# Hyena's convolution chain: the elementwise work on one engine, two butterfly levels summed in PSUM, and the channels in halves

## The chip, the cores and the metric

The kernel runs on one core of a Trainium2 chip. The metric is the device time of one execution in microseconds. Three runs of the kernel before gave 2783.18, 2772.97 and 2788.09 us, so its median is 2783.18 us. One more execution was taken with the hardware profiler, and all rows below come from it.

TensorE multiplies matrices into PSUM banks. VectorE (DVE in the rows), GpSimd (POOL) and ScalarE (ACT) do the elementwise work, and SyncE (SP) issues most loads. A tile of 128 partitions by 1024 fp32 numbers is the usual unit.

## What is computed

The reference is a trunk of two layers over 1024 tokens with 1024 channels. Layer 0 adds two mixers, a Hyena long convolution and a differential attention with rotary positions; layer 1 is a gated position mixer; each layer ends with a feed-forward part with a short convolution. The change concerns the Hyena part and, in one table, the rotary products:

```python
def hyena_mix(proj, ...):                       # proj: 1024 x 1536
    v, x1, x2 = jnp.split(dwconv3(proj, conv_w, conv_b), 3, axis=-1)
    filt = hyena_filters(L, w1, b1, freq, w2, b2, w3)   # 2 orders, 2L taps, 512 channels
    z = v
    for o, gate in enumerate((x1, x2)):
        z = gate * fftconv_bidir(z, filt[:, o], d_skip[o])
    return z
# fftconv_bidir: y = irfft(rfft(u, 2L) * rfft(h, 2L))[:L]
```

So two convolutions stand in a row for each channel, and the second needs the gated result of the first.

## The kernel before, in words

The function `layer0_front` holds all of it, from the start to the first scores of the attention at about 675 us. Its TensorE work is of two kinds: projections (`conv_mtile` for Hyena's three inputs, `proj_v`, `proj_kc`, `proj_qk`), which take each fp32 operand as a high and a low part (tiles `hh`, `hl`, `whi`, `wlo`, results in `pj`), and Fourier matmuls in plain fp32 (tables `tbf` forward, `tbi` inverse, results in `pf`). A plain fp32 matmul shows as two records in the trace.

A transform over 2048 points is split in two: an 8-point butterfly over tile rows `r`, and 128-point matmuls. `dft` does the forward one: 16 matmuls, a level of sums and differences out of PSUM (one ScalarE copy, then an addition and a subtraction on VectorE for each of the real and imaginary part `c`), and two further levels on SBUF tiles `f`. `spectrum` multiplies by the filter's spectrum, loaded from DRAM. `idft` does three levels of sums and differences and returns two tiles `q0`, `q1`; `conv_chain` then runs the inverse matmuls on them and multiplies by the gate. `conv_chain(half)` does this for order 0 and order 1, for 256 channels at a time, so that there are four such steps, called chain steps here. `filters` makes the eight filter parts (order x half of the channels x direction) with `dft_part` and stores their spectra.

Strings such as `F_DFT`, `F_INV`, `F_PART`, `F_SP` and `F_ROPE` give the engine of each elementwise operation in turn, V for VectorE and G for GpSimd. `F_W` does so for the low parts of the weights (`wlo`). The helpers `add`, `sub` and `mul` show as line 132 in the profile, `stt` (a scaled addition) as 128, `mm` as 154.

`eager(main(), side())` fixes the order in which the work is written down: `side` (all filters, then the chain of both halves) goes on until it lacks an input, then `main` (the projections: v, context keys, Hyena's, queries and keys) goes on by one unit. A scheduler then orders each engine's instructions by readiness, and what stands under `first()` goes ahead. The tiles come from pools: seven buffers of the 2048-column tiles `f`, two of the PSUM tiles `pj` and two of `pf`.

Of the kernel before, what the change touches and what calls it, by code (L numbers as in the profile page):

```python
# [20 lines left out]
P = 128  # L21
# [19 lines left out]
F_DFT, F_INV = ("VGVGVVVGVVVGVGVVVG", "VGVGVVVGVVVGVGVVVG", "VGVGVVVGVVVGVGVVVG", "VGVGVVVGVVVGGGVVVG"), ("VGVVVVGGVGVVVGGGVVGVGVVGG", "VGVVVVGGVGVVVGGGVVGVGVVGG", "VGVVVVGGVGVVVGGGVVGVGVVGG", "VGVVVVGVVGVVVGGGVVGVGVVGG")  # L41
F_PART = ("VGGGVGGVVVVVG", "VGGVVGGVVVVVV", "VGGGVGGVVVVVG", "VGGVVGGVVVVVV", "VGGGVGGVVVVVG", "VGGVVGGVVVVVV", "VGGGVGGVVVVVG", "VGGVVGGVVVVVV")
F_SP = ("GGVVVV", "GGVVVV", "GGVVVV", "GGVVVV", "GGVVVV", "GGVVVV", "GGVVVV", "GGVVVV")
F_W = ("GGGGGGGGGGGG", "GGGG", "VGGG", "VGGVVGGG")
F_ROPE = ("GVVG", "GVVV", "GVVG", "VVVG", "GVVG", "GVVG", "GVVV", "GVGG")
# [47 lines left out]
def tile_kernel(ctx: ExitStack, tc: tile.TileContext, ap: dict, out: bass.AP, stop=None):  # L93
# [194 lines left out]
    def layer0_front(fp):  # L288
        with ExitStack() as es:
# [141 lines left out]
            def dft(z, n):  # L431

                e = turns(F_DFT[n])
                a, b = f8(), f8()
                for c in range(2):
                    g1 = fwd(z, c, 1)
                    A.copy(out=b[:, c], in_=g1)
                    g0 = fwd(z, c, 0)
                    add(V, a[:, c], g0, b[:, c])
                    sub(V, b[:, c], g0, b[:, c])  # L440
                    yield
# [63 lines left out]
            def filters():  # L505
                h2r = h2s.rearrange("p (s r) -> p r s", r=8)
                for o in range(2):
                    raw = f8()
                    w3, w3s = raw.rearrange("p a b n -> p a (b n)")[:64, 0], None
                    w3 = raw[:64, 0].rearrange("p (a b) n -> p a (b n)", a=2)  # L510
                    w3s = raw[:64, 1].rearrange("p (a b) n -> p a (b n)", a=2)
                    ld(w3, ap["hy_w3"][:, o])
                    add(V, w3s[:, 0], w3[:, 0], w3[:, 1])
                    sub(V, w3s[:, 1], w3[:, 0], w3[:, 1])
                    ws = f8(F32R)
                    w3h = ws[:, 0].rearrange("p (a b) n -> p a (b n)", a=2)
                    w3l = ws[:, 1].rearrange("p (a b) n -> p a (b n)", a=2)
                    A.copy(out=w3h[0:64], in_=w3s)
                    A.copy(out=w3h[64:128], in_=w3s)
                    sub(V, w3l[0:64], w3s, w3h[0:64])  # L520
                    sub(V, w3l[64:128], w3s, w3h[0:64])
                    for half in range(2):
                        win = h8(ap["window"][half], (1, 8))[:, 0]
                        cs = slice(half * CH, (half + 1) * CH)
                        dsk = tp.tile([P, CH], F32, tag="dsk", name=nm("dsk"), bufs=1)
                        ld(dsk[0:1], ap["dskip"][o : o + 1, cs])
                        for sd in range(2):
                            z = f8z()
                            for g in range(2):
                                ps = ps4()  # L530
                                for r in range(4):
                                    mm(ps[:, r], h2r[:, g * 4 + r], w3h[:, sd, cs], True, False)
                                    mm(ps[:, r], h2r[:, g * 4 + r], w3l[:, sd, cs], False, True)
                                gs = slice(g * 4, g * 4 + 4)
                                mul(V, z[:, gs], ps, win[:, gs])
                            if sd == 0:

                                p0 = ps2("pf")
                                mm(p0[:, :CH], h2r[:, 0], w3h[:, 1, cs], True, False)
                                mm(p0[:, :CH], h2r[:, 0], w3l[:, 1, cs], False, True)  # L540
                                f0 = tp.tile([P, CH], F32, tag="f0", name=nm("f0"), bufs=1)
                                mul(V, f0[0:1], p0[0:1, :CH], win[0:1, 0])
                                add(V, f0[0:1], f0[0:1], z[0:1, 0])
                                V.tensor_scalar(out=f0[0:1], in0=f0[0:1], scalar1=0.5, scalar2=None, op0=MUL)
                                stt(V, z[0:1, 0], dsk[0:1], 1.0 / S, f0[0:1], MUL, ADD)
                            yield
                            X = yield from dft_part(z, sd, 2 * o + half)
                            for par in range(2):
                                st(Hd[o, half, par][:, sd * 1024 : (sd + 1) * 1024],
                                   X[:, par].rearrange("p a b -> p (a b)"))  # L550
                            yield
# [20 lines left out]
            def idft(Y, n):  # L572

# [29 lines left out]
                q0, q1 = f8(), f8()  # L603
                add(e(), q0[:, :, 0], E[:, :, 0], O[:, :, 0])
                sub(e(), q1[:, :, 0], E[:, :, 0], O[:, :, 0])
                stt(V, q0[:, :, 1::2], O[:, :, 1::2], RT2, E[:, :, 1::2], MUL, ADD)
                stt(V, q1[:, :, 1::2], O[:, :, 1::2], -RT2, E[:, :, 1::2], MUL, ADD)
                add(e(), q0[:, 0, 2], E[:, 0, 2], O[:, 1, 2])
                sub(e(), q0[:, 1, 2], E[:, 1, 2], O[:, 0, 2])
                sub(e(), q1[:, 0, 2], E[:, 0, 2], O[:, 1, 2])  # L610
                add(e(), q1[:, 1, 2], E[:, 1, 2], O[:, 0, 2])
                return q0, q1

            def conv_chain(half):
# [3 lines left out]
                for o in range(2):  # L618
# [7 lines left out]
                    if o == 0:  # L626
                        xg = h8(x1d[half].rearrange("p a b -> p (a b)"), (1, 8))[:, 0]
                        z = f8z()
                        for g in range(2):
                            ps = ps4()  # L630
                            for r in range(4):
                                for c in range(2):
                                    mm(ps[:, r], tbi[:, c, g * 4 + r], q[g][:, c, r], c == 0, c == 1)
                            gs = slice(g * 4, g * 4 + 4)
                            mul(V, z[:, gs], ps, xg[:, gs])
                            yield
                    else:
# [83 lines left out]
            def proj_hyena():  # L721
# [23 lines left out]
                for half in range(2):  # L745
                    for kind in range(3):
                        for j in range(2):
                            a = conv_mtile(4 * kind + 2 * half + j)
                            if pend:
                                post(*pend)  # L750
                            pend = (half, kind, j, a)
                            yield
# [1121 lines left out]
```

## Time and profile before

| | before |
|---|---|
| median of three runs | 2783.18 us |
| the profiled execution | 2781.85 us, its span 2780.1 us |
| TensorE busy | 2488.7 us (90%) |
| VectorE busy | 1803.7 us (65%) |
| GpSimd busy | 1264.8 us (45%) |
| ScalarE busy | 1205.2 us (43%) |

The shares are means over the whole span. The front stage is the first quarter of it, and the slices, windows and timelines below show it apart. A row of a group gives line, engine, operation, the tile written and the tiles read, the shapes, the count, the busy time with the mean of one in ns, and the idle time just before them with what ended it. In a timeline the two numbers in front are start and length, and the brackets hold the idle time before and its releaser.

### The profile page before, as it was taken

To read this page: it belongs to the slowest core of one execution; us is meant where nothing else is said; L and a number is where in the kernel's file an instruction comes from. 1 tells how busy PE (TensorE), PEld (TensorE's weight loads), DVE (VectorE), ACT (ScalarE), POOL (GpSimd) and SP (SyncE) were. 2 spreads that over 40 slices of the span, in tenths; PEclk is the share of its full clock that TensorE was granted. 3 is DMA by queue.
4 is the path that set the end of the run, shared out by engine and by line. 5 is a ranking of instruction groups with operands and counts; after the bars stand their busy time and mean duration, and the time that the engine had idled before them with its cause. 6 is when DMAs were issued, how large, how long until landed. Compare 5 with 4: busy or idle time off the path is not lost. (4 is left out here: it accounts for less than half of the span.)

```text
span 2780.1 us, 30586 instructions
## 1 busy us (share of the span) xinstructions
PE 2488.7 (90%) x11192; PEld 1981.5 (71%) x11192; DVE 1803.7 (65%) x2021; ACT 1205.2 (43%) x1871; POOL 1264.8 (45%) x917
## 2 busy tenths in 40 slices
PE   6799667767988889999999999999999999999897
PEld 2798556655767766777777777778877777787676
DVE  4676787874998376656666876642367665566854
ACT  2322111113767255555555444512257565665342
POOL 1333654545444163332323776613343433338775
PEclk9899888888999989999999999999999999999998
DMA  7134131235761265788878833311335777779422
GB/s 279 65 111 158 38 121 39 90 128 181 227 188 50 73 204 129 206 206 216 217 205 227 294 121 110 113 38 48 142 88 125 175 181 170 173 160 319 144 80 99
DMA packets 166855, 412.76 MB, mean 148 GB/s; under 512 B 16011, under 2 KB 28815, under 8 KB 164528
## 3 DMA queue, kind: packets, MB, share of 16 engines
q1 hardware_dynamic: 86352, 248.76, 27.9%
q0 software_dynamic: 34848, 63.45, 13.4%
q10 hardware_dynamic: 45504, 98.58, 9.6%
q8 instruction: 88, 1.44, 0.2%
q14 instruction: 63, 0.52, 0.1%
HBM read 261.31 MB, written 85.98 MB: 125 GB/s over the span
## 5 line engine op out<-in xcount | busy, mean ns | idle before, releaser
L154 PE MATMUL b<-u,u 128*128 128x512 f32 (+1 forms) x5624 | 1331.1, 396 | 65.2 <-POOL u L132 23.8
L154 PEld LDWEIGHTS b<-u,u 128*128 128x128 f32 x5624 | 1063.1, 192 | 331.4 <-POOL u L132 34.1
L132 DVE TENSOR_TENSOR u<-u,u 128x512 fp32r<-128x512 f32 (+2 forms) x470 | 464.5, 1014 | 337.9 <-ACT u L1141 178.9
L132 POOL TENSOR_TENSOR u<-u,u 128x512 fp32r<-128x512 f32 (+1 forms) x338 | 504.6, 1514 | 298.5 <-ACT u L1141 183.9
L1152 POOL DMA_DIRECT2D u<-u x242 | 211.3, 920 | 491.9 <-ACT u L1151 378.7
L1141 ACT CAST u<-u 128x512 fp32r<-128x512 f32 x462 | 261.7, 616 | 238.6 <-DVE u L132 96.0
L154 PE MATMUL b<-x,u 128*128 128x512 f32 x1224 | 296.8, 397 | 0.8 <-DMA u<-u 0.8
L128 DVE SCALAR_TENSOR_TENSOR u<-u,cols,u 128x1023 f32<-128x1023 f32 x176 | 232.3, 1326 | 93.2 <-ACT u L1588 85.2
L154 PEld LDWEIGHTS b<-x,u 128*128 128x128 f32 x1224 | 229.5, 188 | 61.9 <-issue 3.4
L132 POOL TENSOR_TENSOR f<-f 128x256 f32<-128x256 f32 (+2 forms) x99 | 124.7, 1273 | 209.9 <-DVE f L132 180.7
L1150 ACT CAST u<-u 128x512 fp32r<-128x512 f32 x242 | 146.1, 614 | 117.7 <-DVE u L132 89.6
L1151 ACT ACTIVATE u<-u 128x512 fp32r<-128x512 f32 x242 | 149.3, 628 | 67.2 <-POOL u L132 60.3
L132 DVE TENSOR_TENSOR f<-f 128x256 f32<-128x256 f32 (+3 forms) x176 | 177.2, 1055 | 1.1
L132 DVE TENSOR_TENSOR u<-u,b 128x512 f32<-128x512 f32 (+1 forms) x132 | 112.2, 859 | 71.5 <-PE b L154 66.7
L154 PE MATMUL pj<-hh,whi 128*128 128x512 f32 x320 | 132.7, 415 | 24.2 <-DVE t L128 14.0
L1588 ACT ACTIVATE u<-u,cols 128x1024 f32<-128x1024 f32 x88 | 109.3, 1242 | 90.2 <-DVE u L132 89.4
L128 DVE SCALAR_TENSOR_TENSOR x<-b,mods,x 128x512 f32<-128x512 f32 (+1 forms) x104 | 88.7, 905 | 68.4 <-PE b L154 68.4
L154 PE MATMUL pj<-hh,wlo 128*128 128x512 f32 x320 | 130.2, 407 | 3.2 <-POOL wlo L132 1.6
L154 PE MATMUL pj<-hl,whi 128*128 128x512 f32 x320 | 131.3, 410 | 0.0
L132 POOL TENSOR_TENSOR p<-p,p 128x1280 f32<-128x1280 f32 x27 | 79.4, 2944 | 94.1 <-ACT p L885 75.3
L874 ACT ACTIVATE p<-s,nx 128x1280 f32<-128x1280 f32 x64 | 85.0, 1328 | 42.0 <-DVE nx L870 39.2
L147 ACT CAST whi<-wraw 128x1024 fp32r<-128x1024 f32 x28 | 29.3, 1049 | 160.5 <-PE pj L154 138.5
(229 smaller groups left out, 3218.3 us busy)
## 6 DMA issues: line engine op xcount, KB each, us to landing
u<-u POOLq DMA_DIRECT2D x242, 256.0 KB, 4.6
u<-wup SPq DMA_DIRECT2D x88, 512.0 KB, 4.9
Td<-u ACTq DMA_DIRECT2D x66, 512.0 KB, 5.5
u<-Td SPq DMA_DIRECT2D x56, 512.0 KB, 4.4
wraw<-modw SPq DMA_DIRECT2D x48, 512.0 KB, 5.5
u<-wdown SPq DMA_DIRECT2D x40, 512.0 KB, 6.1
wraw<-modw0b SPq DMA_DIRECT2D x32, 512.0 KB, 4.6
xs<-x ACTq DMA_DIRECT2D x48, 256.0 KB, 2.0
```

What stands on the lines that cost most here:

```text
L128: eng.scalar_tensor_tensor(out=o, in0=a, scalar=sc, in1=b, op0=op0, op1=op1)
L132: eng.tensor_tensor(out=o, in0=a, in1=b, op=op)
L147: A.copy(out=hi, in_=x)
L154: T.matmul(o, l, r, start=st and not onto, stop=sp, skip_group_check=onto)
L874: A.activation(q.p[m], q.s, AF.Exp, bias=q.nx, accum_out=q.l[:, m : m + 1])
L1141: A.copy(out=t[:, H0], in_=x)
L1150: A.copy(out=t[:, H0], in_=x)
L1151: A.activation(t[:, H1], t[:, H0].bitcast(F32), AF.Copy, scale=-1.0)
L1152: G.dma_start(out=t[:, H1], in_=x, accum_op=ADD)
L1588: A.activation(a, c, AF.Identity, bias=col(f"fb{l}", f), scale=col(f"fw{l}1", f))
```

## The change

Four things change in `layer0_front`.

First, the tables of the chain and of the rotary products name VectorE throughout. Those of the filter parts and of the weights' low parts stay.

Second, `dft` negates four of its eight input rows on ScalarE into a tile `zn`, and lets TensorE add up both terms of the first level in PSUM: 32 matmuls instead of 16, four ScalarE copies instead of two, and no additions out of PSUM. Third, `idft` no longer forms `q0` and `q1`. ScalarE scales the odd part and a negated copy of it, and the inverse matmuls, twice as many, add up the last level in PSUM.

Fourth, `filters` and `proj_hyena` take a half of the channels as an argument. The main order is now Hyena's first half, v, context keys, Hyena's second half, queries and keys; the side order is the filters and the chain of the first half, then those of the second. The filters' last weights are loaded and split for each half.

```diff
+F_DFT, F_INV = ("V" * 18,) * 4, ("V" * 25,) * 4
...
-F_ROPE = ("GVVG", "GVVV", "GVVG", "VVVG", "GVVG", "GVVG", "GVVV", "GVGG")
+F_ROPE = ("VVVV",) * 8
...
                 e = turns(F_DFT[n])
                 a, b = f8(), f8()
+                zn = t4().rearrange("p (r n) -> p r n", r=4)
+                A.activation(zn, z[:, 4:8], AF.Copy, scale=-1.0)
                 for c in range(2):
-                    g1 = fwd(z, c, 1)
-                    A.copy(out=b[:, c], in_=g1)
-                    g0 = fwd(z, c, 0)
-                    add(V, a[:, c], g0, b[:, c])
-                    sub(V, b[:, c], g0, b[:, c])
+                    for o, z1 in ((a, z[:, 4:8]), (b, zn)):
+                        ps = ps4()
+                        for r in range(4):
+                            mm(ps[:, r], tbf[:, c, r], z[:, r], True, False)
+                            mm(ps[:, r], tbf[:, c, 4 + r], z1[:, r], False, True)
+                        A.copy(out=o[:, c], in_=ps)
                     yield
...
-            def filters():
+            def filters(half):
...
-                    ld(w3, ap["hy_w3"][:, o])
...
+                    w3, w3s = (raw[:64, i, 0:2] for i in range(2))
+                    ld(w3, ap["hy_w3"][:, o, :, cs])
...
                 yield
-                q0, q1 = f8(), f8()
-                add(e(), q0[:, :, 0], E[:, :, 0], O[:, :, 0])
-                sub(e(), q1[:, :, 0], E[:, :, 0], O[:, :, 0])
-                stt(V, q0[:, :, 1::2], O[:, :, 1::2], RT2, E[:, :, 1::2], MUL, ADD)
-                stt(V, q1[:, :, 1::2], O[:, :, 1::2], -RT2, E[:, :, 1::2], MUL, ADD)
-                add(e(), q0[:, 0, 2], E[:, 0, 2], O[:, 1, 2])
-                sub(e(), q0[:, 1, 2], E[:, 1, 2], O[:, 0, 2])
-                sub(e(), q1[:, 0, 2], E[:, 0, 2], O[:, 1, 2])
-                add(e(), q1[:, 1, 2], E[:, 1, 2], O[:, 0, 2])
-                return q0, q1
+                n = f8()
+                for r, w in ((0, 1.0), (1, RT2)):
+                    A.activation(n[:, :, r::2], O[:, :, r::2], AF.Copy, scale=-w)
+                A.activation(O[:, :, 1::2], O[:, :, 1::2], AF.Copy, scale=RT2)
+
+                def terms(g, c, r):
+                    if r == 2:
+                        o = (O, n)[g ^ c][:, 1 - c, 2]
+                    else:
+                        o = (O, n)[g][:, c, r]
+                    return E[:, c, r], o
+
+                return terms
...
                                 for c in range(2):
-                                    mm(ps[:, r], tbi[:, c, g * 4 + r], q[g][:, c, r], c == 0, c == 1)
+                                    for i, x in enumerate(q(g, c, r)):
+                                        mm(ps[:, r], tbi[:, c, g * 4 + r], x, c + i == 0, c + i == 2)
                             gs = slice(g * 4, g * 4 + 4)
                             mul(V, z[:, gs], ps, xg[:, gs])
...
-                                        mm(ps[:, rs], q[g][:, c, r, j * P : (j + 1) * P], tbi[:, c, g * 4 + r],
-                                           c == 0, c == 1)
+                                        for i, x in enumerate(q(g, c, r)):
+                                            mm(ps[:, rs], x[:, j * P : (j + 1) * P], tbi[:, c, g * 4 + r],
+                                               c + i == 0, c + i == 2)
...
+            def proj_hyena(half):
...
-                for half in range(2):
...
             def main():
-                for gen in (proj_v(), proj_kc(), proj_hyena(), proj_qk()):
+                for gen in (proj_hyena(0), proj_v(), proj_kc(), proj_hyena(1), proj_qk()):
                     yield from gen
 
             def side():
-                yield from filters()
                 ld(tbi, ap["dfti"])
                 for half in range(2):
+                    yield from filters(half)
                     yield from conv_chain(half)
                 done.add("side")
 
```

The first place is on TensorE, where the matmuls of the filters' parts stand. In these rows `pf` tiles with `h2s` or `tbf` are filter matmuls, `pj` tiles are products of a projection. Before, in the middle of a part:

```order
L154 MATMUL pf_661<-f_105_638,tbf 128x256 x4
L154 MATMUL pf_667<-f_105_638,tbf 128x256 x4
L154 MATMUL pj_1278<-whi_1268,hl_346 128x256
L154 MATMUL pj_1278<-whi_1268,hh_351 128x256
L154 MATMUL pj_1278<-wlo_1269,hh_351 128x256
L154 MATMUL pj_1278<-whi_1268,hl_352 128x256
L154 MATMUL pj_1278<-whi_1268,hh_357 128x256
L154 MATMUL pj_1278<-wlo_1269,hh_357 128x256
L154 MATMUL pj_1278<-whi_1268,hl_358 128x256
L154 MATMUL pj_1278<-whi_1274,hh_363 128x256
L154 MATMUL pj_1278<-wlo_1275,hh_363 128x256
L154 MATMUL pf_674<-f_105_638,tbf 128x256 x3
```

After, at the end of the first half's four parts (the last row belongs to the chain's first transform):

```order
L154 MATMUL pf_649<-f_91_562,h2s 128x256 x8
L154 MATMUL pf_659<-f_91_562,h2s 128x256 x8
L154 MATMUL pf_671<-f_107_648,tbf 128x256 x4
L154 MATMUL pf_677<-f_107_648,tbf 128x256 x4
L154 MATMUL pf_684<-f_107_648,tbf 128x256 x3
L154 MATMUL pf_689<-f_107_648,tbf 128x256 x3
L154 MATMUL pj_1034<-hh_339,whi_1030 128x512
L154 MATMUL pj_1034<-hl_340,whi_1030 128x512
L154 MATMUL pj_1034<-hh_339,wlo_1031 128x512
L154 MATMUL pj_1034<-hh_345,whi_1030 128x512
L154 MATMUL pj_1034<-hl_346,whi_1030 128x512
L154 MATMUL pf_916<-f_129_841,tbf 128x256 x8
```

Nine products stood between the matmuls of one part; now the first half's parts follow one another closely, and five products lie between the last of them and the transform.

The second place is on VectorE, from the end of one inverse to the next transform (`f_242`, then `f_147`, are odd parts of the inverse; `pf` are the banks that the gate multiplies). Before:

```order
L128 SCALAR_TENSOR_TENSOR f_242_1922<-f_251_1959 128x256
L132 TENSOR_TENSOR f_242_1922<-f_251_1959 128x256 x2
L132 TENSOR_TENSOR f_252_1968<-f_239_1903,f_242_1922 128x2x256
L128 SCALAR_TENSOR_TENSOR f_252_1968<-f_242_1922,f_239_1903 128x4x256
L128 SCALAR_TENSOR_TENSOR f_253_1969<-f_242_1922,f_239_1903 128x4x256
L132 TENSOR_TENSOR f_252_1968<-f_239_1903,f_242_1922 128x256 x2
L132 TENSOR_TENSOR f_269_2122<-pf_2123,h_268_2120 128x1024
L132 TENSOR_TENSOR f_269_2122<-pf_2133,h_268_2120 128x1024
L132 TENSOR_TENSOR f_272_2143<-pf_2151,f_273_2144 128x1024
L132 TENSOR_TENSOR f_273_2144<-pf_2151,f_273_2144 128x1024
L132 TENSOR_TENSOR f_272_2143<-pf_2164,f_273_2144 128x1024
L132 TENSOR_TENSOR f_273_2144<-pf_2164,f_273_2144 128x1024
```

After:

```order
L132 TENSOR_TENSOR f_147_978<-f_155_1010 128x2x256 x2
L132 TENSOR_TENSOR f_156_1015<-f_155_1010 128x256 x4
L132 TENSOR_TENSOR f_147_978<-f_156_1015 128x256 x3
L128 SCALAR_TENSOR_TENSOR f_147_978<-f_156_1015 128x256
L132 TENSOR_TENSOR f_173_1172<-pf_1173,h_172_1170 128x1024
L132 TENSOR_TENSOR f_173_1172<-pf_1191,h_172_1170 128x1024
L128 SCALAR_TENSOR_TENSOR t_202_1380<-pj_1331,cols,t_202_1380 128x1023 x2
L132 TENSOR_TENSOR f_183_1253<-f_176_1209 128x2x512 x2
L132 TENSOR_TENSOR f_184_1256<-f_183_1253 128x2x256 x2
```

The last level of the inverse (the four rows that read `f_239` and `f_242`) and the transform's four rows that read `pf` and `f_273` are gone; the two gate rows remain, with two tap additions of a projection behind them.

The third place is on TensorE, between the inverse matmuls (`tbi`) and the next transform's (`tbf`). Before:

```order
L154 MATMUL pf_2123<-f_252_1968,tbi 128x256 x2
L154 MATMUL pf_2133<-f_253_1969,tbi 128x256
L154 MATMUL pf_2123<-f_252_1968,tbi 128x256 x4
L154 MATMUL pf_2133<-f_253_1969,tbi 128x256 x6
L154 MATMUL pj_2255<-hh_339,whi_2251 128x512
L154 MATMUL pj_2255<-hl_340,whi_2251 128x512
L154 MATMUL pj_2255<-hh_339,wlo_2252 128x512
L154 MATMUL pj_2255<-hh_345,whi_2251 128x512
L154 MATMUL pj_2255<-hl_346,whi_2251 128x512
L154 MATMUL pj_2255<-hh_345,wlo_2252 128x512
L154 MATMUL pj_2255<-hh_351,whi_2251 128x512
L154 MATMUL pf_2145<-f_269_2122,tbf 128x256 x4
```

After (the first three rows are the end of the inverse's matmuls):

```order
L154 MATMUL pf_1191<-f_157_1024,tbi 128x256
L154 MATMUL pf_1191<-f_144_959,tbi 128x256
L154 MATMUL pf_1191<-f_157_1024,tbi 128x256
L154 MATMUL pf_1213<-f_173_1172,tbf 128x256
L154 MATMUL pj_1331<-hl_376,whi_1327 128x512
L154 MATMUL pj_1331<-hh_375,wlo_1328 128x512
L154 MATMUL pj_1331<-hh_381,whi_1327 128x512
L154 MATMUL pj_1331<-hl_382,whi_1327 128x512
L154 MATMUL pj_1331<-hh_381,wlo_1328 128x512
L154 MATMUL pf_1213<-f_173_1172,tbf 128x256 x7
L154 MATMUL pf_1223<-f_173_1172,tbf 128x256
L154 MATMUL pf_1223<-t_178_1211,tbf 128x256
```

Inverse and transform now each read two kinds of tile by turns, the plain and the scaled or negated one, and five products lie between them where seven were.

## Rows read from the trace of the kernel before

**Rows 1.** Busy tenths in the page's 40 slices: TensorE and VectorE

```profile
PE   6799667767988889999999999999999999999897
...
DVE  4676787874998376656666876642367665566854
```

**Rows 2.** Windows: stretch, its length, busy time of each engine, clock, DMA

```profile
74.00:664.00 590.00, 468.41 (x2284) 402.38 (x2285) 435.61 (x407) 106.56 (x114) 280.59 (x162) 0.89 0.29 99
106.00:289.00 183.00, 174.06 (x965) 158.23 (x964) 120.82 (x158) 38.70 (x44) 56.22 (x50) 0.99 0.35 120
289.00:355.00 66.00, 42.05 (x174) 34.16 (x175) 61.32 (x49) 8.27 (x9) 43.50 (x24) 0.83 0.21 69
364.00:433.00 69.00, 42.35 (x184) 34.57 (x184) 63.32 (x49) 9.50 (x9) 44.95 (x24) 0.80 0.27 92
525.00:593.00 68.00, 43.35 (x191) 35.93 (x190) 62.71 (x50) 7.21 (x7) 42.90 (x23) 0.84 0.17 61
```

**Rows 3.** TensorE's waits, 289 to 606 us: total, times, longest

```profile
PE pf L154 <- DVE f L132: 55.8, 4, 23.1
...
PE pj L682 <- DVE t L128: 18.6, 3, 10.4
```

**Rows 4.** Timeline of TensorE, six places: start us, length us, instruction, [idle before]

```profile
289.08 5.45 PE L154 MATMUL pf<-f,tbf 128*128 128x256 f32 x24 [2.06 <-ACT f L734]
...
352.50 3.78 PE L154 MATMUL pf<-f,tbi 128*128 128x256 f32 x8 [15.80 <-DVE f L132]
...
448.57 7.13 PE L154 MATMUL pf<-f,tbf 128*128 128x256 f32 x24 [2.06 <-ACT f L734]
...
589.89 2.07 PE L154 MATMUL pf<-tbi,f 128*128 128x128 f32 x8 [23.11 <-DVE f L132]
...
604.60 0.50 PE L154 MATMUL pj<-hh,whi 128*128 128x512 f32 x1 [1.83 <-ACT t L773]
...
663.26 1.30 PE L154 MATMUL s<-f,f 128*128 128x512 f32 x6
```

**Rows 5.** Timeline of VectorE, four places

```profile
109.27 1.22 DVE L132 TENSOR_TENSOR f<-pf,h 128x1024 f32<-128x1024 f32 x1 [8.34 <-PE pf L154]
...
181.68 0.67 DVE L132 TENSOR_TENSOR f<-f 64x512 f32<-64x512 f32 x1
...
366.90 2.48 DVE L132 TENSOR_TENSOR f<-pf,f 128x1024 f32<-128x1024 f32 x2 [3.91 <-PE pf L154]
...
381.40 0.41 DVE L132 TENSOR_TENSOR f<-f 128x256 f32<-128x256 f32 x1
...
381.73 1.27 DVE L128 SCALAR_TENSOR_TENSOR t<-pj,cols,t 128x1023 f32<-128x1023 f32 x1
```

**Rows 6.** VectorE by form: first chain step 289 to 355; the last row, 60 to 106

```profile
L132 DVE TENSOR_TENSOR f<-f 128x1024 f32<-128x1024 f32 x7 | 12.5, 1807 | 0.0
...
L132 DVE TENSOR_TENSOR f<-f,f 128x256 f32<-128x256 f32 x2 | 0.7, 410 | 0.0
...
L132 DVE TENSOR_TENSOR f<-f,f 128x512 f32<-128x512 f32 x1 | 0.7, 677 | 0.0
...
L132 DVE TENSOR_TENSOR hl<-t,hh 128x1024 fp32r<-128x1024 f32 x5 | 5.9, 1215 | 0.0
```

**Rows 7.** GpSimd by form, 289 to 593 us

```profile
L132 POOL TENSOR_TENSOR wlo<-wraw,whi 128x1024 fp32r<-128x1024 f32 x10 | 28.9, 2893 | 31.0 <-ACT whi L147 31.0
```

**Rows 8.** TensorE by form, 289 to 606 us

```profile
L154 PE MATMUL pf<-f,tbf 128*128 128x256 f32 x128 | 31.3, 397 | 4.1 <-ACT f L734 4.1
...
L154 PE MATMUL pf<-f,tbi 128*128 128x256 f32 x64 | 18.0, 451 | 30.4 <-DVE f L132 30.4
...
L154 PE MATMUL pf<-tbi,f 128*128 128x128 f32 x128 | 17.5, 298 | 25.4 <-DVE f L132 25.4
```

**Rows 9.** Timeline ahead of the attention, 660 to 676 us

```profile
667.16 2.34 POOL L132 TENSOR_TENSOR t<-t,t 128x1024 f32<-128x1024 f32 x1
...
674.47 2.08 PE L154 MATMUL s<-f,f 128*128 128x512 f32 x4 [9.90 <-ACT t L773]
```

More of the change, by code (lines that the diff above doesn't have):

```diff
@@ L40 @@
 BW, LW = 6, 2
-F_DFT, F_INV = ("VGVGVVVGVVVGVGVVVG", "VGVGVVVGVVVGVGVVVG", "VGVGVVVGVVVGVGVVVG", "VGVGVVVGVVVGGGVVVG"), ("VGVVVVGGVGVVVGGGVVGVGVVGG", "VGVVVVGGVGVVVGGGVVGVGVVGG", "VGVVVVGGVGVVVGGGVVGVGVVGG", "VGVVVVGVVGVVVGGGVVGVGVVGG")
+F_DFT, F_INV = ("V" * 18,) * 4, ("V" * 25,) * 4
 F_PART = ("VGGGVGGVVVVVG", "VGGVVGGVVVVVV", "VGGGVGGVVVVVG", "VGGVVGGVVVVVV", "VGGGVGGVVVVVG", "VGGVVGGVVVVVV", "VGGGVGGVVVVVG", "VGGVVGGVVVVVV")
-F_SP = ("GGVVVV", "GGVVVV", "GGVVVV", "GGVVVV", "GGVVVV", "GGVVVV", "GGVVVV", "GGVVVV")
+F_SP = ("V" * 6,) * 8
 F_W = ("GGGGGGGGGGGG", "GGGG", "VGGG", "VGGVVGGG")
-F_ROPE = ("GVVG", "GVVV", "GVVG", "VVVG", "GVVG", "GVVG", "GVVV", "GVGG")
+F_ROPE = ("VVVV",) * 8
 F_H, F_X, F_SQ = "VGVVGVVG", "VVVVVVVV", ("V", "V", "V", "V", "V", "V", "V")
@@ L503, in dft_part @@
                 return X
-            def filters():
+            def filters(half):
                 h2r = h2s.rearrange("p (s r) -> p r s", r=8)
+                cs = slice(half * CH, (half + 1) * CH)
                 for o in range(2):
[L508 to L511, printed above, removed]
-                    ld(w3, ap["hy_w3"][:, o])
+                    raw, ws = f8(), f8(F32R)
+                    w3, w3s = (raw[:64, i, 0:2] for i in range(2))
+                    ld(w3, ap["hy_w3"][:, o, :, cs])
                     add(V, w3s[:, 0], w3[:, 0], w3[:, 1])
                     sub(V, w3s[:, 1], w3[:, 0], w3[:, 1])
-                    ws = f8(F32R)
-                    w3h = ws[:, 0].rearrange("p (a b) n -> p a (b n)", a=2)
-                    w3l = ws[:, 1].rearrange("p (a b) n -> p a (b n)", a=2)
+                    w3h, w3l = (ws[:, i, 0:2] for i in range(2))
                     A.copy(out=w3h[0:64], in_=w3s)
@@ L521, in filters @@
                     sub(V, w3l[64:128], w3s, w3h[0:64])
-                    for half in range(2):
[L523 to L551, printed above, removed]
@@ new lines, in filters @@
+                    win = h8(ap["window"][half], (1, 8))[:, 0]
+                    dsk = tp.tile([P, CH], F32, tag="dsk", name=nm("dsk"), bufs=1)
+                    ld(dsk[0:1], ap["dskip"][o : o + 1, cs])
+                    for sd in range(2):
+                        z = f8z()
+                        for g in range(2):
+                            ps = ps4()
+                            for r in range(4):
+                                mm(ps[:, r], h2r[:, g * 4 + r], w3h[:, sd], True, False)
+                                mm(ps[:, r], h2r[:, g * 4 + r], w3l[:, sd], False, True)
+                            gs = slice(g * 4, g * 4 + 4)
+                            mul(V, z[:, gs], ps, win[:, gs])
+                        if sd == 0:
+                            p0 = ps2("pf")
+                            mm(p0[:, :CH], h2r[:, 0], w3h[:, 1], True, False)
+                            mm(p0[:, :CH], h2r[:, 0], w3l[:, 1], False, True)
+                            f0 = tp.tile([P, CH], F32, tag="f0", name=nm("f0"), bufs=1)
+                            mul(V, f0[0:1], p0[0:1, :CH], win[0:1, 0])
+                            add(V, f0[0:1], f0[0:1], z[0:1, 0])
+                            V.tensor_scalar(out=f0[0:1], in0=f0[0:1], scalar1=0.5, scalar2=None, op0=MUL)
+                            stt(V, z[0:1, 0], dsk[0:1], 1.0 / S, f0[0:1], MUL, ADD)
+                        yield
+                        X = yield from dft_part(z, sd, 2 * o + half)
+                        for par in range(2):
+                            st(Hd[o, half, par][:, sd * 1024 : (sd + 1) * 1024],
+                               X[:, par].rearrange("p a b -> p (a b)"))
+                        yield
@@ L719, in proj_kc @@
                     yield
-            def proj_hyena():
+            def proj_hyena(half):
                 z = {}
@@ L744, in proj_hyena @@
                 pend = None
[L745 to L752, printed above, removed]
+                for kind in range(3):
+                    for j in range(2):
+                        a = conv_mtile(4 * kind + 2 * half + j)
+                        if pend:
+                            post(*pend)
+                        pend = (half, kind, j, a)
+                        yield
                 post(*pend)
```

## The prediction

> **What bounds the kernel now.** I read the page's slices first, each 69.5 us long. From the sixteenth on TensorE is busy nine tenths of nearly every one; in the fifth to ninth (278 to 625 us) it has six or seven tenths, and VectorE seven or eight [rows 1]. The whole change lies there, in the front stage up to about 675 us. A table of windows then takes it apart [rows 2]: from 106 to 289 us TensorE works 174.1 of 183 us, while the filters run beside projections; in a step of the convolution chain (four alike, three stand) VectorE works 61 to 63 us of 66 to 69, TensorE only 42 to 43, GpSimd 43 to 45. So VectorE bounds the steps. The waits say the same: in the chain's stretch TensorE waits 55.8 us, four times, for VectorE's tile f, and 18.6 us for its t [rows 3]. The timelines give the steps' edges. In the first half, the first step's transform goes out at 289.08 [rows 4], VectorE leaves the step at about 355.4, starts the next at 366.90 [rows 5], and TensorE has nothing from the last product to 604.60, when five products remain before the attention [rows 4]. VectorE's steps last 62.5, 66.0, 62.6 and 65.0 us, together 256, with gaps of 11.5 and 11.0 between the two steps of each half. These ends are those of the list of VectorE's instructions; of each kind one row stands [rows 5].
>
> Why are steps so long? By form, VectorE's 128x1024 addition takes 1807 ns in the first step, and 1215 where GpSimd rests; of 128x256 and 128x512 additions 410 and 677 ns stand, undisturbed [rows 6]. Counted at these, the first step holds about 36.8 us of VectorE's work, and it was busy 61.32. The 24.5 us too much stand beside 43.50 us of GpSimd: 0.56 us lost for each us of GpSimd.
>
> The Trainium skill, SBUF — State Buffer, section "🔬 SBUF: two separate sides", says that VectorE and GpSimd share a pair of ports as an exclusive lock: whoever starts first holds it for the whole instruction, and the other blocks. By that the loss would be 1.0 us per us; the row shows about half. The time by it is the fourth case below.
>
> **The change part by part.**
>
> *Tables all on VectorE.* A step's work moves from two engines to one, and GpSimd's share of the chain ends. *Two levels in the banks.* Four 1024-column additions of the transform and the eight of the inverse's last level go away from VectorE and GpSimd. What is left for VectorE in a step: 18 instructions of 128x1024 at 1.215, 8 of 512 at 0.68, 24 of 256 at 0.41, two scaled additions at about 1.27 = 39.7 us. Neighbours overlap: a 0.41 instruction starts at 381.40 and the next at 381.73 [rows 5], 0.08 earlier; 52 times that is 4.2, leaving 35.5. GpSimd keeps only the weight splits, 2.89 us each [rows 7], two in a step: 5.8 x 0.56 = 3.2. That is 38.7 us for a plain step; four tap additions of a projection at 1.2 lie in the first and third, 4.8 more; some 6 us of taps, rotation and splits in the last. Steps: 43.2, 38.4, 43.2, 44.4, together 169 instead of 256. Bounds for the unknown price of the splits: nothing (they would read as the 1215 row), or their whole length; I take 0.56, the measured one.
>
> *The price on TensorE.* Each transform has 32 more records of 256 columns, 128 in all; the inverses 64 more of 256 and 128 more of 128 columns. At the rows' averages, 31.3/128 = 0.245, 18.0/64 = 0.281 and 17.5/128 = 0.137 us [rows 8], this is 31.3 + 18.0 + 17.5 = 67 us. Those averages hold stretches at a low granted clock (0.80 to 0.84 [rows 2]); the undisturbed transform takes 5.45/24 = 0.227 [rows 4]. Half of these matmuls stand where nothing covers them, between the end of one step on VectorE and the start of the next. ScalarE's six more operations per step (about 1.0 us each) lie beside them, but for one scaling and one copy.
>
> *Gap between the two steps of a half, twice.* 60 inverse records that follow VectorE's last operation at 0.227 to 0.281: 13.6 to 16.9. Eight product matmuls between: 1.9. The gate's multiplication 1.2. The 48 transform records that must precede the last copy, at 0.227 to 0.245: 10.9 to 11.8. The copy 1.0. Together 28.6 to 32.8, where before it was 11.5 and 11.0; VectorE idles there, and TensorE has little else.
>
> *After the second inverse.* 128 records at 0.112 (half of 0.227) to 0.137 with the scalings ahead of them, about 3 us: 18 us until TensorE goes on. In the first half 2.5 us of tap additions stand in the way too: 20.5.
>
> *The order by halves.* Before, all eight filter parts lay in a stretch that TensorE filled, 109.27 to 289 [rows 2, 5]. Now four parts precede the chain and four follow its first half. The first four took 72.4 us, from 109.27 to 181.68 [rows 5]. With the second order's weights prepared among them (3.5) and two tap additions (2.4) VectorE ends at 187.6; the last copies of the transform follow, and the first step starts about 7 us later, at 194.5. For the second four I take 81 us: 76.4 us of TensorE's filter and product matmuls, and the weights ahead. Then three products (58.7/5 = 11.7 each, from 604.60 to 663.26 [rows 4]) with two transpositions, 35 to 37 us, and 12 us to the chain's first VectorE operation. The weights' total stays, but in four pieces of half size, so its loads double in number; they are prefetched and I cost them at nothing; if that cover failed, one could cost up to the 8.34 us that VectorE waits ahead of 109.27 [rows 5], once for each half.
>
> *The tail.* Rotation on VectorE: GpSimd's 2.34 us addition [rows 9], and the multiplication ahead of it, become 1.2 us each. The attention's scores begin at 663.26 [rows 4] but stall until 674.47 for ScalarE [rows 9]; I take 7 instead of 11 us.
>
> **Sum.** 194.5 + 43.2 + (28.6 to 32.8) + 38.4 + 20.5 = 325 to 329. Filters 81: 406 to 410. Products and start 47 to 49: 453 to 459. 43.2 + (28.6 to 32.8) + 44.4 + 18 = 134 to 138: 587 to 597. Five products 58.7, tail 7: 653 to 663, against 674.5. The gain is 11 us with everything at the averages, and up to 25 if the matmuls keep 0.227 and fewer product matmuls stand between those of the filters. A second way: the steps' 256 - 169 = 87 us are given back to TensorE, which idles 590 - 468.4 = 122 us from 74 to 664 us [rows 2], and it spends 67 on the new matmuls: 20. I take 17, between the two. What follows 675 us is unchanged. The profiled execution took 2781.85 us (span 2780.1), 1.3 below the median 2783.18. Forecast 2765, its own range 2752 to 2776.
>
> **The rivals.**
>
> 1. *Clean.* Splits cost nothing, no low clock. For it: the 1215 row [rows 6]. Steps 3.2 us shorter each, 12.8, on top of the upper gain of 25: 2744. Against: the granted clock fell in every step where TensorE had gaps [rows 2], and gaps remain.
>
> 2. *The doubled matmuls eat it.* At 448.57 a transform took 7.13/24 = 0.297 [rows 4], after a wait of only 2.06 us. If the gaps' records go at 0.297, and those of 128 columns as much above their average (0.145), a gap is 17.8 + 1.9 + 1.2 + 14.3 + 1.0 = 36.2 where the middle value has 30.7, and an end 2.5 longer: 2 x 5.5 + 2 x 2.5 = 16 us, 2781, no change. Against: the transform of 289.08, after the same wait, took 0.227.
>
> 3. *Slower: TensorE at its lower level in the serial gaps.* After 15.80 us without work the first eight inverse records took 3.78 us, 0.47 each, and after 23.11 us eight of 128 columns 2.07, 0.26 each [rows 4]; that is 1.2 instead of 2.4 GHz. The place is the chain's gaps, where the new matmuls are alone and wait for VectorE first. All of them at the lower level: 120 x 0.47 + 96 x 0.454 + 256 x 0.26 = 167, where the averages give 93: 74 more, 2839; half of it 2802. It decides from about 45%: 32 us above 2765. Against: the 128 transform records have 0.245 in the mean [rows 8], not 0.454, and the idle time ahead of the gaps (24 us of 66 in the first step [rows 2]) shrinks with the steps.
>
> The Trainium skill, TensorE: Matmul & The Clock Gate, section "Loop structure matters more than you think", says that a loop with a long wait ahead of its matmuls runs cold. The rows agree in the 0.47 above; this rival is what it would make of the gaps.
>
> 4. *The lock in full.* Each split costs 2.89 and not 1.6: 2.6 us a step, 10 in all: 2775. Against it the 0.56.
>
> **How the numbers follow.** Forecast 0.45, clean 0.15, doubled matmuls 0.14, low clock 0.19, lock 0.07. What this kernel's measurement can tell from no change is 0.5%, 14 us: faster is below 2769, slower above 2797. Of the forecast's range two thirds lie below 2769, so faster 0.31 + 0.15 and a part of the doubled matmuls' spread, 0.50; slower 0.18; the rest 0.32. The range goes from just below the clean case, 2742, to the half of the low clock, 2800; outside are about 0.08 below and 0.12 above.
>
> **What would show it.** VectorE about 40 us busy per step, its 128x1024 addition near 1215 ns, GpSimd only with splits; gaps of 29 to 33 us between a half's steps, filled with 0.23 to 0.28 us matmuls of tbi and tbf; TensorE's waits for VectorE's f below 40 us; idle TensorE now before 190 us and around the second filters; a scores' stall of 6 to 7 us. Wrong: steps above 50 us (then GpSimd was not what stretched them), matmuls above 0.35 us in the gaps (low clock), or filters of the second half over 90 us.

## The result and the profile after

The changed kernel takes 2745.82 us (four runs, 2741.46 to 2748.75) against 2781.65 us (four runs); the ratio is 0.9872, 95% interval 0.9841 to 0.9903. That is 36 us faster, where 17 were forecast. The profiled execution has a span of 2739.6 us. These are its page's slices, TensorE and VectorE, against [rows 1]: the fifth to ninth TensorE digits were 6, 6, 7, 7, 6 and are now 9, 9, 9, 9, 8.

```profile
PE   6889999988989899999999999999999999999897
...
DVE  4677665678988386665666876541377655566854
```

The windows, for [rows 2] (length, busy time of TensorE, its weight loads, VectorE, ScalarE, GpSimd, clock): first the front stage, then the four chain steps.

```profile
74.00:637.00 563.00, 516.42 (x2602) 449.79 (x2603) 376.64 (x463) 132.52 (x143) 116.47 (x66) 0.95 0.31 104
...
192.00:236.00 44.00, 39.08 (x172) 31.95 (x171) 43.57 (x56) 8.47 (x9) 6.81 (x2) 0.96 0.32 108
261.00:301.00 40.00, 37.24 (x289) 36.60 (x288) 39.77 (x52) 6.78 (x8) 5.72 (x2) 0.96 0.41 139
449.00:494.00 45.00, 39.68 (x175) 32.37 (x174) 43.87 (x56) 8.64 (x10) 7.63 (x2) 0.96 0.31 105
519.00:565.00 46.00, 39.59 (x177) 32.69 (x175) 45.66 (x59) 8.40 (x9) 17.02 (x2) 0.96 0.19 60
```

VectorE still fills its steps, but they last 40 to 46 us and not 62 to 66. TensorE works 37 to 40 us in each where it had 42 of 66, and the clock granted in them is 0.96, not 0.80 to 0.84. VectorE by form in the first step, for [rows 6], shows what changed on VectorE: the 128x1024 addition reads 1315 ns where it read 1807, and 128x256 and 128x512 additions stand at 419 and 685 ns. First these two forms in the first step before, then the three after:

```profile
L132 DVE TENSOR_TENSOR f<-f 128x256 f32<-128x256 f32 x14 | 13.3, 992 | 0.1
...
L132 DVE TENSOR_TENSOR f<-f 128x512 f32<-128x512 f32 x6 | 8.0, 1344 | 0.0
```

```profile
L132 DVE TENSOR_TENSOR f<-f 128x1024 f32<-128x1024 f32 x10 | 12.8, 1315 | 7.9 <-ACT f L443 7.9
...
L132 DVE TENSOR_TENSOR f<-f 128x256 f32<-128x256 f32 x23 | 8.1, 419 | 0.0
L132 DVE TENSOR_TENSOR f<-f 128x512 f32<-128x512 f32 x8 | 5.1, 685 | 0.0
```

VectorE's timeline, for [rows 5], has the edges: the first step from 191.70 to 235.68, the second from 260.62 to 300.87; the third ends at 493.78, the last goes from 518.65 to the end of the row of 564.34. The row of 247.59 is the gate's second multiplication, inside the first gap.

```profile
191.70 8.92 DVE L132 TENSOR_TENSOR f<-f 128x1024 f32<-128x1024 f32 x18 [7.86 <-ACT f L443]
...
235.26 0.42 DVE L128 SCALAR_TENSOR_TENSOR f<-f 128x256 f32<-128x256 f32 x1
...
247.59 1.22 DVE L132 TENSOR_TENSOR f<-pf,h 128x1024 f32<-128x1024 f32 x1 [3.09 <-PE pf L154]
...
260.62 2.36 DVE L132 TENSOR_TENSOR f<-f 128x1024 f32<-128x1024 f32 x2 [6.98 <-ACT f L443]
...
300.46 0.41 DVE L128 SCALAR_TENSOR_TENSOR f<-f 128x256 f32<-128x256 f32 x1
...
493.36 0.42 DVE L128 SCALAR_TENSOR_TENSOR f<-f 128x256 f32<-128x256 f32 x1
...
518.65 3.57 DVE L132 TENSOR_TENSOR f<-f 128x1024 f32<-128x1024 f32 x4 [11.33 <-ACT f L443]
...
564.34 0.41 DVE L128 SCALAR_TENSOR_TENSOR f<-f 128x256 f32<-128x256 f32 x1
```

TensorE's timeline, for [rows 4], in the first gap and at the attention's start: eight inverse records run before VectorE's last operation of the step, the other 52 take 11.38 us, 0.219 each, and the scores stall for 0.30 us.

```profile
232.59 1.89 PE L154 MATMUL pf<-f,tbi 128*128 128x256 f32 x8
...
236.16 11.38 PE L154 MATMUL pf<-f,tbi 128*128 128x256 f32 x52
...
637.83 1.45 PE L154 MATMUL s<-f,f 128*128 128x512 f32 x6 [0.30 <-ACT t L777]
```

Three more windows of the changed kernel, in the columns of those above: the first gap, the last inverse, and the five products ahead of the attention.

```profile
235.68:260.62 24.94, 24.94 (x118) 21.82 (x117) 5.02 (x5) 8.24 (x8) 2.36 (x1) 1.00 0.24 85
566.99:581.73 14.74, 14.74 (x108) 14.74 (x109) 6.37 (x7) 2.07 (x2) 0.00 (x0) 0.81 0.58 198
581.73:636.23 54.50, 54.50 (x244) 45.15 (x242) 40.25 (x37) 14.04 (x14) 4.80 (x2) 1.00 0.60 192
```

TensorE by form, 74 to 637 us, for [rows 8]; and its costliest wait in the front stage, for [rows 3], which was 55.8 us in the chain alone:

```profile
L154 PE MATMUL pf<-f,tbf 128*128 128x256 f32 x416 | 102.3, 390 | 6.7 <-DVE f L132 2.9 <-ACT f L739 2.1 <-ACT f L482 1.8
...
L154 PE MATMUL pf<-tbi,f 128*128 128x128 f32 x256 | 35.6, 307 | 8.8 <-ACT f L606 4.4 <-DVE f L132 4.2
L154 PE MATMUL pf<-f,tbi 128*128 128x256 f32 x128 | 28.8, 381 | 2.1 <-DVE f L132 2.1
L154 PE MATMUL pf<-t,tbf 128*128 128x256 f32 x64 | 19.0, 379 | 0.0
```

```profile
PE pf L154 <- DVE f L132: 12.1, 7, 4.2
```

The attention's scores run on from 637.83 us, and from 674.47 before [rows 9]: of the 40.5 us between the spans of the two profiled executions (2780.1 and 2739.6), 36.6 stand in the front stage.

### The profile page after: what moved, and what is told of

Its sections match the earlier page's. It is cut to its first block, busy times and chain, and to the rows that moved or that the text cites. A ratio compares the mean times of both kernels' runs of the same rounds, so it can differ in the third digit from the quotient of the medians.

```text
span 2739.6 us, 31153 instructions
## 1 busy us (share of the span) xinstructions
PE 2528.1 (92%) x11512; PEld 2022.3 (74%) x11512; DVE 1753.7 (64%) x2079; ACT 1230.0 (45%) x1899; POOL 1093.4 (40%) x819
## 5 line engine op out<-in xcount | busy, mean ns | idle before, releaser
L132 POOL TENSOR_TENSOR wlo<-wraw,whi 128x1024 fp32r<-128x1024 f32 x24 | 75.9, 3170 | 313.7 <-ACT whi L147 220.6
L132 DVE TENSOR_TENSOR f<-f 128x256 f32<-128x256 f32 (+3 forms) x236 | 152.2, 705 | 38.9 <-ACT f L443 36.3
L154 PE MATMUL pf<-f,tbf 128*128 128x256 f32 x416 | 102.3, 390 | 6.7 <-DVE f L132 2.9
```

The costliest lines, as they stand in the source:

```text
L132: eng.tensor_tensor(out=o, in0=a, in1=b, op=op)
L154: T.matmul(o, l, r, start=st and not onto, stop=sp, skip_group_check=onto)
```

## The experiments

"Banks" are the two butterfly levels summed in PSUM. Times are medians, ratios are to the kernel before on the same chip.

**The rotary table of before.**

```diff
-F_ROPE = ("VVVV",) * 8
+F_ROPE = ("GVVG", "GVVV", "GVVG", "VVVG", "GVVG", "GVVG", "GVVV", "GVGG")
```

> The changed kernel with the rotary table of before, all else changed. Theory A (the surplus over the forecast is partly the tail, where the last rotation on GpSimd held the attention's scores): the stall before the scores, 0.3 us now and 9.9 before, comes back with 5 to 10 us, and the time goes from 2745.8 to about 2754. Rival (the scores start early because the order by halves leaves other work last): within 3 us of the changed kernel.

2751.88 us, 0.9899 (0.9867 to 0.993). The stall is back as in [rows 9], behind GpSimd's 3.31 and 2.34 us:

```profile
642.74 3.31 POOL L132 TENSOR_TENSOR t<-t,f 128x1024 f32<-128x1024 f32 x1 [2.99 <-DVE t L778]
...
646.13 2.34 POOL L132 TENSOR_TENSOR t<-t,t 128x1024 f32<-128x1024 f32 x1
...
653.44 2.50 PE L154 MATMUL s<-f,f 128*128 128x512 f32 x6 [9.93 <-ACT t L777]
```

The mechanism is shown by the row; the 6 us of the medians lie within the two intervals. The scores run on 15.6 us later than in the changed kernel (653.44 against 637.83), and most of that is not in the total.

**The chain's tables of before.**

```diff
-F_DFT, F_INV = ("V" * 18,) * 4, ("V" * 25,) * 4
-F_SP = ("V" * 6,) * 8
+F_DFT, F_INV = ("VGVGVVVGVVVGVGVVVG", ...), ("VGVVVVGGVGVVVGGGVVGVGVVGG", ...)
+F_SP = ("GGVVVV", ...)
```

> The changed kernel with the transform, inverse and spectrum tables of before, so that GpSimd again does its share of the chain; banks, order and rotation stay changed. Theory A (GpSimd's help costs VectorE 0.56 us per us, so it is worth little): VectorE's work in a step falls by about 13 us at lone durations and loses about 15 us to some 27 us of GpSimd, steps of 46 to 50 instead of 44, time 2750 to 2762. Rival B (the tables carry the gain): steps of 55 to 60 and 2770 or more. Rival C (GpSimd helps once its share is small): steps below 42 and 2740.

2811.94 us, 1.0109 (1.0081 to 1.0137): slower than before the change. Theory A's steps came true, its time did not: from VectorE's first to its last operation of a step 49.6, 49.6, 49.3 and 50.2 us pass, and the time is 50 us above its range; it lies where rival B had it, without rival B's steps. First the first step's edges; then windows of the first two steps, with the tap additions that follow them, and of the stretch between the second and third step (its last row is the changed kernel's same stretch); then VectorE by form in the first step:

```profile
192.85 1.23 DVE L132 TENSOR_TENSOR f<-f 128x1024 f32<-128x1024 f32 x1 [7.87 <-ACT f L443]
...
241.70 0.75 DVE L132 TENSOR_TENSOR f<-f 128x256 f32<-128x256 f32 x2
```

```profile
193.00:246.00 53.00, 33.26 (x137) 26.64 (x136) 49.36 (x38) 8.87 (x9) 38.19 (x20) 0.81 0.07 23
269.00:324.00 55.00, 31.38 (x198) 28.54 (x197) 48.30 (x40) 8.36 (x9) 37.21 (x19) 0.81 0.22 76
324.00:493.00 169.00, 159.66 (x957) 146.15 (x957) 67.82 (x91) 34.22 (x39) 40.68 (x31) 0.97 0.29 102
301.00:449.40 148.40, 139.94 (x818) 128.04 (x817) 72.82 (x94) 33.79 (x39) 35.62 (x28) 0.99 0.29 100
```

```profile
L132 DVE TENSOR_TENSOR f<-f 128x1024 f32<-128x1024 f32 x7 | 14.5, 2116 | 8.0 <-ACT f L443 7.9
L132 DVE TENSOR_TENSOR f<-f 128x256 f32<-128x256 f32 x14 | 11.7, 880 | 2.4 <-POOL f L132 2.3
...
L128 DVE SCALAR_TENSOR_TENSOR t<-pj,cols,t 128x1023 f32<-128x1023 f32 x4 | 5.1, 1277 | 1.0 <-ACT t L677 0.9
```

GpSimd is busy 37 to 38 us in a step and does not shorten it: VectorE has 38 instructions left of the changed kernel's 56 and is busy 49.4 us, not 43.6. Its instructions on SBUF tiles are stretched again, the tap additions that read PSUM (`pj`) keep their 1277 ns, and TensorE's clock is back at 0.81. I had sized GpSimd's share at 27 us; it is 38, two weight splits of 5.7 included. The steps explain 24 us of the 66. Another 26 lie between the second and third step (174.5 us for 148.5), 11 after the last step, the rest in the gaps and at the start. The 26 are mostly matmuls that had run in the first two steps: there TensorE has 335 records where it had 461, and between the halves 957 where it had 818. In the second of them it waits 12.1 us for ScalarE's `whi` and 7.9 for GpSimd's `wlo`, the high and low parts of weights.

**The order of before.**

```diff
-                for gen in (proj_hyena(0), proj_v(), proj_kc(), proj_hyena(1), proj_qk()):
+                for gen in (proj_v(), proj_kc(), proj_hyena(), proj_qk()):
...
-                ld(tbi, ap["dfti"])
+                yield from filters()
+                ld(tbi, ap["dfti"])
                 for half in range(2):
-                    yield from filters(half)
                     yield from conv_chain(half)
```

> The changed kernel with all filters ahead of the chain and the projections in the old order; tables and banks stay changed. Theory A (what counts is that VectorE's steps are shorter; the order is worth little): 2740 to 2752. Rival (the order by halves carries the gain, since it gives TensorE products to fill the chain of the first half and keeps its clock up): 2765 or more, with TensorE idle over 80 us up to the attention instead of 42.

2753.34 us, 0.9897 (0.9869 to 0.9926), just above theory A's range. By the medians the order is worth 8 us, but the intervals overlap, and the scores begin at 638.17 us, 2 us later than in the changed kernel (636.23). TensorE idles 53 us up to them, not over 80, so the rival falls.

**The banks undone.**

```diff
-                    for o, z1 in ((a, z[:, 4:8]), (b, zn)):
-                        ps = ps4()
...
+                    add(V, a[:, c], g0, b[:, c])
+                    sub(V, b[:, c], g0, b[:, c])
...
-                    return E[:, c, r], o
+                return q0, q1
```

> The changed kernel with both butterfly levels back on VectorE, out of PSUM, and half the transform and inverse matmuls; tables and order stay changed. Theory A (what the banks take off VectorE, about 10 us a step, comes back on TensorE in the gaps): steps of 54 instead of 44, gaps of 13 instead of 25, the end after the second inverse 8 us shorter: 2745 to 2752. Rival (the banks carry the gain): 2765 or more.

2722.81 us, 0.9795 (0.9768 to 0.9822): the banks cost 23 us, and my theory had none. The front stage is shorter though VectorE does more:

```profile
74.00:609.00 535.00, 459.90 (x2286) 397.36 (x2286) 418.58 (x512) 108.72 (x120) 111.26 (x67) 0.93 0.33 111
```

TensorE is busy 459.9 and not 516.4 us; it idles 75 instead of 47, so half of the 56 us come back.

**Only the transform's level, and only the inverse's level, undone.** The edits are the first and the second half of the one above.

> The changed kernel with only the transform's first level back on VectorE (16 matmuls per transform instead of 32). Theory A (after the change TensorE is what bounds the front stage, idle only 47 of 563 us, so a matmul record costs its time there, while VectorE has slack): 128 records at 0.216 = 28 us less on TensorE, four additions of 1.22 us a step = 20 us more on VectorE, of which about half shows: 2730 to 2738. Rival (the two bank levels only pay or cost together): within 5 us of 2746.

> The changed kernel with only the inverse's last level back on VectorE (half of the inverse matmuls). Theory A: 64 records at 0.216 and 128 at 0.112 = 28 us less on TensorE, 5 us a step more on VectorE, 21 in all: 2730 to 2738, so that this and the transform's level together make the 23 us that undoing both gave. Rival (the inverse's last level in the banks is worth it, and the transform's alone costs): 2746 to 2755.

2742.61 us, 0.9861 (0.9841 to 0.9882), and 2738.99 us, 0.9843 (0.9824 to 0.9862). Together they give 23 us, alone 3 and 7; the first misses the range of 2730 to 2738, the second by 1 us. Neither is told apart from the changed kernel, and the intervals leave open whether 3 and 7 are really less than 23. The traces, one execution each, point that way: the scores run on from 640.31 and 626.82 us, and from 609.73 with both undone, against 637.83. In this order:

```profile
640.31 2.70 PE L154 MATMUL s<-f,f 128*128 128x512 f32 x12
...
626.82 1.43 PE L154 MATMUL s<-f,f 128*128 128x512 f32 x6 [2.33 <-ACT t L772]
...
609.73 1.49 PE L154 MATMUL s<-f,f 128*128 128x512 f32 x6 [2.53 <-ACT t L769]
```

With only the transform's level undone, TensorE's waits in the front stage are:

```profile
PE pf L154 <- DVE f L132: 28.4, 10, 12.9
PE pj L154 <- POOL wlo L132: 18.1, 4, 14.3
```

In the changed kernel they are 12.1 and 4.0. TensorE's 27 us less of work up to the scores (489.8 against 516.9) turned into 30 us of these two waits.

**Only the tables, on the kernel before.**

```diff
+F_DFT, F_INV = ("V" * 18,) * 4, ("V" * 25,) * 4
+F_SP = ("V" * 6,) * 8
+F_ROPE = ("VVVV",) * 8
```

> The kernel before with only the chain's and the rotation's tables on VectorE; banks and order as before. Theory A (GpSimd beside VectorE stretches VectorE's instructions; with it gone a step is about 50 us, not 64): four times 13 us of VectorE's time, less about 8 that the order by halves brings: 2725 to 2735. Rival (the tables need the order by halves, since TensorE waits for the chain's end anyway): 2755 or more.

2727.74 us, 0.98 (0.9777 to 0.9823). Three tables give 55 us, more than the whole change. This kernel differs from the changed one without the banks (2722.81) in the order alone, and the two are not told apart.

**Only the banks, on the kernel before.** The edit is that of the banks undone, the other way.

> The kernel before with only the two levels in the banks; tables (the inverse's shorter one read from its start) and order as before. Theory A (the banks cost more on TensorE than they free while GpSimd still takes part): 2790 to 2815, since undoing the tables alone gave 2812. Rival (they pay where VectorE is the bound, as it is here): 2760 to 2775.

2801.1 us, 1.0074 (1.005 to 1.0097). The banks cost here too, 18 us, where VectorE is the bound of the steps. Tables alone and banks alone add up to -37 us; the whole change measured -36.

**Extra GpSimd work that reads, and that only writes.**

```diff
                 add(e(), E[:, 1, 3], t[:, 1, 2], t[:, 0, 3])
+                dmy = tp.tile([P, 768], F32, tag="dmy", name=nm("dmy"), bufs=1)
+                for _ in range(6):
+                    add(G, dmy.rearrange("p (r n) -> p r n", r=3), E[:, 0, 0:3], E[:, 1, 0:3])
```

In the second kernel one `G.tensor_copy` of a column and twelve `G.memset(dmy, 0.0)` stand in place of the loop.

> The changed kernel with six extra GpSimd additions of 128x768 in each chain step, which read the inverse's even part twice and write a tile that nothing uses; about 2.2 us each, 13 a step, 53 in all. Theory A (VectorE loses about 0.56 us per us of a GpSimd instruction that reads two tiles): steps of 50 to 53 instead of 44 to 46, VectorE's 128x512 and 128x256 instructions beside them near double their 0.68 and 0.41, time 2765 to 2780. Rival (the tables' gain was not GpSimd's presence but its slowness on the chain's own work): VectorE's durations stay, time within 8 us of 2746.

> The changed kernel with twelve GpSimd memsets of 128x768 in each chain step at the same place, which write a tile that nothing uses and read none; about 0.9 us each. If only GpSimd instructions that read cost VectorE time: steps as without them, 44 to 46, and 2742 to 2750. If any busy GpSimd does: steps of 48 to 51 and 2760 to 2775.

One run each: 2782.75 and 2740.41 us, 3 above and 2 below the ranges expected. The first step lasts 53.6 us in the reading kernel and 44.0, as in the changed one, in the writing kernel. VectorE by form, first step, while the extra instructions ran; the reading kernel first, then the writing one:

```profile
L132 DVE TENSOR_TENSOR f<-f 128x1024 f32<-128x1024 f32 x2 | 5.6, 2838 | 0.0
L132 DVE TENSOR_TENSOR f<-f 128x256 f32<-128x256 f32 x4 | 4.8, 1228 | 0.0
L132 DVE TENSOR_TENSOR f<-f 128x512 f32<-128x512 f32 x2 | 4.4, 2232 | 0.0
```

```profile
L132 DVE TENSOR_TENSOR f<-f 128x256 f32<-128x256 f32 x11 | 3.8, 416 | 0.0
L132 DVE TENSOR_TENSOR f<-f 128x1024 f32<-128x1024 f32 x2 | 2.3, 1210 | 0.0
L132 DVE TENSOR_TENSOR f<-f 128x512 f32<-128x512 f32 x3 | 2.0, 686 | 0.0
```

Six additions on GpSimd, 13.86 us in that step, stretch 17 VectorE instructions from 8.57 to 18.18 us: 0.69 us per us. Twelve memsets, 9.51 us, cost nothing: beside them the same 17 take 8.57 us again. In order the reading kernel's GpSimd and VectorE rows, the changed kernel's VectorE row, and the memsets:

```profile
229.09 13.86 POOL L132 TENSOR_TENSOR dmy<-f 128x768 f32<-128x768 f32 x6 [4.23 <-DVE f L132]
```

```profile
227.07 18.18 DVE L132 TENSOR_TENSOR f<-f 128x512 f32<-128x512 f32 x17
```

```profile
226.77 8.57 DVE L132 TENSOR_TENSOR f<-f 128x512 f32<-128x512 f32 x17
```

```profile
227.31 9.51 POOL L589 MEMSET dmy<- 128x768 f32 x12
```

The step grows by 9.6 us, and four of these make the 37 us of the time. A GpSimd instruction that reads only one tile was not tried.

**More on VectorE, without the banks.** On the kernel with the banks undone, first the low parts of Hyena's weights, then the filter parts too.

```diff
-F_W = ("GGGGGGGGGGGG", "GGGG", "VGGG", "VGGVVGGG")
+F_W = ("VVVVVVVVVVVV", "GGGG", "VGGG", "VGGVVGGG")
...
+F_PART = ("V" * 13,) * 8
```

> The version without the banks (2722.8) with the low parts of Hyena's weights on VectorE too. Theory A (a split on GpSimd costs VectorE 0.56 x 2.9 = 1.6 us, on VectorE itself 1.22): 12 x 0.4 = 5 us at most, 2717 to 2723. Rival (TensorE then waits for splits that stand behind the chain's work in VectorE's queue): 2728 or more.

> As the one before, with the filter parts' elementwise work on VectorE as well. Theory A: 40 GpSimd instructions of 0.80 in the mean become 40 of 0.41 on VectorE, 16 us more work and about 18 less lost, in a stretch where VectorE waits 56 us for TensorE: 2712 to 2722. Rival (the filters are a serial chain for VectorE, so what is added shows): 2725 to 2735.

2717.24 us, 0.9779 (0.9752 to 0.9807), and 2709.98 us, 0.9746 (0.972 to 0.9771). The second, 2 us below its range, beats both kernels: 36 us less than the changed one, its interval clear of it. The first is in its range and not told apart from the kernel without the banks.

## Why the prediction was half the size

The direction was right, and so was the mechanism of the tables; the size was off: 17 us forecast, 36 measured, so that 2745.82 lies below the forecast's own range of 2752 to 2776. By the sum's terms, from the timelines:

- *Steps.* Forecast 43.2, 38.4, 43.2, 44.4; measured 44.0, 40.3, 44.4, 46.1. The term is 5.6 us too low in all: the prediction works out 38.7 for a plain step and then adds 38.4, and the 128x1024 additions, some of them beside splits, still read 1315 and not 1215 ns.
- *TensorE's price.* Forecast 67 us. Measured (102.3 + 19.0 - 84.2) + (28.8 - 18.0) + (35.6 - 17.5) = 66.0, with 84.2 the transform row of before over the same stretch, 352 records, filters included. Right.
- *The gaps.* The first term that failed. Forecast 28.6 to 32.8, measured 24.9 twice (235.68 to 260.62, 493.78 to 518.65): 11.6 us against the middle value. I had taken the averages of [rows 8] as one end. They hold stretches at a clock of 0.80 to 0.84, in which TensorE waited for VectorE; now TensorE works all 24.94 us of the gap, the clock is 1.00, and the records take 0.219. That is about half of the miss. The lower end, at 0.227, is still 3.7 us too long, so the other half is the path: eight of the sixty inverse records ran before VectorE's last operation (232.59), and the gate's second multiplication (247.59) lay beside products, where the sum had it as a term of its own.
- *After the last step.* The second. Forecast 18 + 58.7 + 7 = 83.7, measured 637.83 - 564.76 = 73.1. Of the 10.6, 5.4 are the tail, mis-sized as 7 where 1.6 pass (636.23 to 637.83): the stall of 9.9 went to 0.3 us, and the rotary run brought it back in full. Another 4.2 are the five products, 54.5 us without a wait at a clock of 1.00. The inverse ahead of them took 17.0 of 18; here, after a wait of 4.14 us, the clock was 0.81.
- *Filters and start.* First step 194.5 forecast, 191.70 measured; from the second step's end to the end of the second filters on VectorE 101.5 and 97.9; from there to the third step 48 and 50.6. Within 4 us each.

These make 2.8 + 11.6 + 10.6 + 3.6 - 2.6 - 5.6 = 20 us, the difference in the attention's start. The second way of the sum (87 us back, 67 spent, 20 gained) came a little closer, but it missed the same thing: TensorE's busy time in the front stage grew from 469.0 (74 to 674 us) to 516.4, 47 and not 66 us; its idle time fell by 84 (131 to 47), nearly the 87. By form the rest of its work in the front stage is 11 us shorter, the products most of all; the other 8 come from the count, since the 66 are a sum of record lengths that overlap in time, and the busy time has an overlap once.

The rivals: the *clean* case had the time (2744) and one of its two reasons, the clock. That the splits cost nothing is not borne out. *Low clock* and *doubled matmuls* fell with the gap's 1.00 and 0.219 us a record. *The lock* deserves more than it got. The Trainium skill, SBUF — State Buffer, section "🔬 SBUF: two separate sides", says that the lock holds for a VectorE instruction with two SBUF inputs only against a GpSimd instruction that reads SBUF. The trace agrees: additions stretch VectorE to 2838 ns, memsets leave it at 1210, and tap additions out of PSUM keep 1277 beside 38 us of GpSimd. The loss is 0.56 to 0.69 us per us and not 1; in the reading kernel eight VectorE instructions pass six of GpSimd. That they go by turns, each waiting for about one, would fit these counts; the runs do not show it.

What the prediction did not ask is which part brings the gain. Its own terms held the answer: the banks take some 10 us a step off VectorE (four additions of 1.22, and of the inverse's eight some 5), 41 in all, and put 67 on TensorE, half of it where nothing covers it. Shown by runs: tables alone -55 us, banks +18 on the kernel before and +23 in the changed one, the order 5 to 8 by the medians and not clear of the intervals. Banks and tables were credited with one common term, so that the one hid the other's loss.

Open: why the weight split comes 14.3 us late when only the transform's level is undone; and why the time after the scores' start differs by some 10 us between kernels (2739.6 - 637.8 = 2102 in the changed one, 2721.0 - 609.7 = 2111 without the banks), so that not all of the front stage's 28 us arrive. Over all kernels it goes from 2094 to 2113, one execution each.

## What to carry to other kernels

Before sharing elementwise work between VectorE and GpSimd, compare an instruction's duration beside GpSimd and alone; here, at a loss of some 0.6 us per us and with GpSimd about twice as long on the same form (2.34 us against 1.22 for the rotation's 128x1024 addition), the second engine shortened nothing. Price each part of a combined change on its own, with the sign it would have alone. Averages of matmul durations belong to the waiting around them: where a change removes the waiting, take the undisturbed row.

## What the runs showed of the hardware

GpSimd busy with memsets cost VectorE nothing (416, 686 and 1210 ns beside 9.51 us of them), GpSimd busy with two-input additions made the same forms 2.3 to 3.3 times as long (1228, 2232, 2838). The granted clock of the front stage went with TensorE's idle time: 0.89 with 131 us idle (before), 0.91 with 109 (tables of before), 0.93 with 75 (banks undone), 0.95 with 47 (changed).
